# Attention scores on one core: PSUM buffers tied to engines, casts moved to GpSimd, whole memsets, transposes spread over five tiles

## The chip, the cores and the metric

One core of a Trainium2 chip. The metric is device time in microseconds (us) for one execution, median of several. Before: 204.12 us (204.04 to 204.3, 3 runs). "Faster" or "slower" needs 2%, about 4.1 us.

## The reference

```python
# q, k: (8, 8, 512, 64) float32
def reference(q, k):
    scale = 1.0 / np.sqrt(q.shape[-1])
    return (np.einsum('bhqd,bhkd->bhqk', q, k) * scale).astype(np.float32)
```

The inputs have 16.8 MB, the output 67.1 MB. All arithmetic on q and k is in bf16, sums and output are fp32.

## The kernel before

Four units (v) of two batches each; a unit has eight output tiles (n) of 128 x 8 x 512 fp32, 2 MB each. Each unit's k and q are loaded as one 2 MB tile apiece, cast to bf16, transposed on TensorE (PE) through PSUM, the buffer that TensorE writes to, copied to SBUF, the on-chip memory (kT, and qz with zeros in the half that the other head uses), and multiplied. The scores leave PSUM with the scale applied (an evacuation), by ScalarE (ACT) or VectorE (DVE) in turn, and are stored by one queue on SyncE (SP).

```python
    raw_pool = ctx.enter_context(tc.tile_pool(name="raw", bufs=3))
    ...
    out_pool = ctx.enter_context(tc.tile_pool(name="out", bufs=4))
    tpsum_pool = ctx.enter_context(tc.tile_pool(name="tpsum", bufs=2, space=bass.MemoryType.PSUM))
    psum_pool = ctx.enter_context(tc.tile_pool(name="psum", bufs=3, space=bass.MemoryType.PSUM))
    ...
    def evacuate(dst, src):
        nonlocal n_evac
        if n_evac % 2 == 0:
            pinned(nc.scalar.mul(out=dst, in_=src, mul=scale))
        else:
            pinned(nc.vector.tensor_scalar(out=dst, in0=src, scalar1=scale, ...))
        n_evac += 1

    def load_and_cast(v):
        both = []
        for src in (k_r, q_r):
            xf = raw_pool.tile([P, 2, J * D], f32, name="xf")
            nc.sync.dma_start(out=xf, in_=src[v])
            xb = bf_pool.tile([P, J, 2, D], bf16, name="xb")
            for s in range(2):
                if v == 0 and src is k_r:
                    copy = (nc.vector.tensor_copy, nc.scalar.copy)[s]
                else:
                    copy = nc.gpsimd.tensor_copy
                pinned(copy(out=xb[:, :, s, :], in_=xf[:, s].rearrange(...)))
            both.append(xb)
        return both
    ...
    for v in range(UNITS):
        ahead = transpose(v + 1, *cast[v + 1]) if v + 1 < UNITS else iter(())
        per_step = 3 if v == 0 else 1      # steps of the next unit's transposes per evacuation
        for n in range(N):
            take(ahead, 1)
            for _ in scores(v, n):         # two matmuls, one evacuation; the store after the fourth
                take(ahead, per_step)
```

`pinned` keeps an engine's instructions in this order. All loads are issued before all stores, on one queue. The fourth load waits until the first raw buffer has been cast.

Of the kernel before, what the change touches and what calls it, by code (L numbers as in the profile page):

```python
# [1 line left out]

# [5 lines left out]


@with_exitstack  # L10
def kernel(
    ctx: ExitStack,
    tc: tile.TileContext,
    q: bass.AP,
    k: bass.AP,
    out: bass.AP,
):






    nc = tc.nc
    B, H, S, D = q.shape
    scale = 1.0 / (D ** 0.5)
    P = 128
    UNITS = B // 2
    N = H
    M = P // (2 * H)  # L30
    R = S // M
    J = R // 2
    RO = 8
    U = S // RO
    JJ = J // RO
    IW = 8 // JJ

    f32 = mybir.dt.float32
    bf16 = mybir.dt.bfloat16

    q_r = q.rearrange("(v b) g (m j) d -> v (b g m) (j d)", b=2, j=R)
    k_r = k.rearrange("(v b) g (m j) d -> v (b g m) (j d)", b=2, j=R)
    out_r = out.rearrange("(v b) (n h) (u i) k -> v (b n) (h u) (i k)", b=2, h=2, i=RO)

    consts = ctx.enter_context(tc.tile_pool(name="consts", bufs=1))
    raw_pool = ctx.enter_context(tc.tile_pool(name="raw", bufs=3))
    bf_pool = ctx.enter_context(tc.tile_pool(name="bf", bufs=5))
    t_pool = ctx.enter_context(tc.tile_pool(name="t", bufs=2))
# [5 lines that stand above are left out]
    pinned = tc.keep_in_program_order  # L54

    n_evac = 0
    n_tp = 0

    def evacuate(dst, src):
        nonlocal n_evac  # L60
        if n_evac % 2 == 0:
            pinned(nc.scalar.mul(out=dst, in_=src, mul=scale))  # L62
        else:
            pinned(nc.vector.tensor_scalar(out=dst, in0=src, scalar1=scale, scalar2=None,  # L64
                                           op0=mybir.AluOpType.mult))
        n_evac += 1

    def half(h):
        return slice(h * D, (h + 1) * D)
# [6 lines that stand above are left out]
            nc.sync.dma_start(out=xf, in_=src[v])  # L76
            xb = bf_pool.tile([P, J, 2, D], bf16, name="xb")
            for s in range(2):
                if v == 0 and src is k_r:
                    copy = (nc.vector.tensor_copy, nc.scalar.copy)[s]  # L80
                else:
                    copy = nc.gpsimd.tensor_copy
                pinned(copy(out=xb[:, :, s, :], in_=xf[:, s].rearrange("p (j d) -> p j d", j=J)))  # L83
            both.append(xb)
        return both

    def clear(qz, h):

        nc.vector.memset(qz[half(h), :, :, (1 - h) * U:(2 - h) * U], 0.0)  # L89

    def rearrange(tp, pattern, dst):

        nonlocal n_tp
        copy = (nc.vector.tensor_copy, nc.scalar.copy)[n_tp % 2]
        n_tp += 1
        for s in range(2):
            src = tp[half(s)].rearrange(pattern, n=N, h=2)
            for h in range(2):
                pinned(copy(out=dst(s, h), in_=src[:, h]))  # L99
                yield  # L100

    def transpose(v, kb, qb):


        kT = t_pool.tile([P, N, M, 2, J], bf16, name="kT")
        qz = qzs[v % 2]
        ts[v] = (kT, qz)
        for j0 in range(0, J, 8):
            tp = tpsum_pool.tile([P, 8, P], bf16, name="tp")
            for j in range(8):  # L110
                pinned(nc.tensor.transpose(out=tp[:, j, :], identity=identity,  # L111
                                           in_=kb[:, j0 + j].rearrange("p s d -> p (s d)")))
            yield
            yield from rearrange(tp, "d j (n h m) -> d h n m j",
                                 lambda s, h: kT[half(h), :, :, s, j0:j0 + 8])
        for i0 in range(0, RO, IW):
            tp = tpsum_pool.tile([P, IW, JJ, P], bf16, name="tp")
            for i in range(IW):
                for jj in range(JJ):
                    pinned(nc.tensor.transpose(out=tp[:, i, jj, :], identity=identity,  # L120
                                               in_=qb[:, RO * jj + i0 + i].rearrange("p s d -> p (s d)")))
            yield
            yield from rearrange(tp, "d i jj (n h m) -> d h i n m jj",
                                 lambda s, h: qz[half(h), i0:i0 + IW, :, h * U:(h + 1) * U]
                                 .rearrange("d i n (m s jj) -> d s i n m jj", s=2, jj=JJ)[:, s])

    def scores(v, n):

        kT, qz = ts[v]
        o = out_pool.tile([P, RO, S], f32, name="o")  # L130
        for i in range(0, RO, 2):
            ps = psum_pool.tile([P, 2, S], f32, name="ps")
            for w in range(2):
                pinned(nc.tensor.matmul(out=ps[:, w, :], lhsT=qz[:, i + w, n, :],  # L134
                                        rhs=kT[:, n].rearrange("d m s j -> d (m s j)"),
                                        start=True, stop=True))
            evacuate(o[:, i:i + 2, :], ps)
            yield
        src = o.rearrange("p i k -> p (i k)")
        nc.sync.dma_start(out=out_r[v, n], in_=src)  # L140

    def take(steps, count):
        for _ in range(count):
            next(steps, None)

    identity = consts.tile([P, P], dtype=bf16)
    make_identity(nc, identity)
    qzs = [consts.tile([P, RO, N, P], bf16, name=f"qz{n}") for n in range(2)]
    for qz in qzs:
        for h in range(2):  # L150
            clear(qz, h)
    cast = [load_and_cast(v) for v in range(UNITS)]

    ts = {}
    for _ in transpose(0, *cast[0]):
        pass
    for v in range(UNITS):
        ahead = transpose(v + 1, *cast[v + 1]) if v + 1 < UNITS else iter(())

        per_step = 3 if v == 0 else 1  # L160
        for n in range(N):
            take(ahead, 1)
            for _ in scores(v, n):
                take(ahead, per_step)
        for _ in ahead:
            pass


# [1 line left out]
_INS = ['q', 'k']  # L170
_OUTS = [((8, 8, 512, 512), 'float32')]


# [23 lines left out]
```

## Time and profile before

| | before |
|---|---|
| time, median | 204.12 us |
| span in the profile | 202.3 us |
| DVE / PE / ACT / POOL busy | 64% / 52% / 51% / 13% |
| DMA queue, share of 16 engines | 97.7% |
| moved | 83.89 MB in 40 transfers of 2 MB |
| evacuations waiting for a store to free a tile | 79.4 us (ACT 50.9, DVE 28.5) |

A busy share is an average over the span. The row of 40 slices: the digit is the busy share in tenths, and 9 stands for 90% or more.

### The profile page before, as it was taken

The numbers are of one execution on the slowest core, as the hardware profiler recorded it, in microseconds if no ns is written. First come the engines' busy times: TensorE is split into PE (matmuls) and PEld (weight loads), VectorE is DVE, ScalarE is ACT, GpSimd is POOL, SyncE is SP. The second block draws the span as 40 slices with busy tenths as digits, with TensorE's granted clock in tenths as the row PEclk, the third lists the DMA queues.
The fourth block names the chain that finished last, engine by engine and source line by source line (L and its number), as shares of the span: only waits on it lengthen the run. The fifth ranks groups of instructions, "written<-read, shape, count | busy, mean of one in ns | idle before, by whom it ended". The sixth has DMA issues, their size and how long they took to land.

```text
span 202.3 us, 1549 instructions
## 1 busy us (share of the span) xinstructions
PE 106.1 (52%) x512; PEld 50.2 (25%) x512; DVE 129.6 (64%) x133; ACT 102.5 (51%) x130; POOL 26.8 (13%) x20
## 2 busy tenths in 40 slices
PE   0045557755854755858575575656564677642000
PEld 0034424432211322423222233223121222210000
DVE  6875669987765686878787788777544455553000
ACT  2254457967654448484756666574833344442000
POOL 1037775756000000000000000000000000000000
PEclk9999999978799699797979787896969655695555
DMA  6999999999999999999999999999999999999991
GB/s 214 428 441 428 424 441 421 424 395 434 437 421 434 432 423 431 434 428 428 437 424 431 431 424 434 434 428 431 434 428 428 431 434 428 428 437 429 416 447 75
DMA packets 5768, 83.99 MB, mean 415 GB/s; under 512 B 640, under 2 KB 640, under 8 KB 640
## 3 DMA queue, kind: packets, MB, share of 16 engines
q1 hardware_dynamic: 5760, 83.89, 97.7%
q8 instruction: 4, 0.07, 0.1%
q14 instruction: 4, 0.03, 0.0%
HBM read 16.78 MB, written 67.11 MB: 415 GB/s over the span
## 4 chain that ended last, share of the span: by engine, by line
DMA 52%; ACT 13%; DVE 13%; PE 10%; issue 2%; ACTq 0%; DVEq 0%; SPq 0%
DMA out_dram<-o 52%; ACT o L62 6%; DVE o L64 5%; PE ps L134 5%; ACT qz L99 4%; DVE qz L89 3%; ACT kT L99 3%; PE tp L120 3%; DVE kT L99 3%; PE tp L111 2%; DVE xb L83 1%; DVE qz L99 1%; ACTq L62 0%; DVEq L64 0%; SPq L140 0%
## 5 line engine op out<-in xcount | busy, mean ns | idle before, releaser
L134 PE MATMUL ps<-kT,qz 128*128 128x512 bf16 x256 | 87.3, 470 | 52.4 <-ACT o L62 43.3
L64 DVE TENSOR_SCALAR o<-ps 128x1024 f32<-128x1024 f32 x64 | 78.2, 1225 | 44.1 <-DMA out_dram<-o 28.5
L62 ACT ACTIVATE o<-ps 128x1024 f32<-128x1024 f32 x64 | 63.5, 1022 | 64.3 <-DMA out_dram<-o 50.9
L134 PEld LDWEIGHTS <-qz 128*128 128x128 bf16 x256 | 28.6, 115 | 98.6 <-issue 87.2
L83 POOL CAST xb<-xf 128x2048 bf16<-128x2048 f32 x14 | 26.1, 1893 | 21.5 <-DMA xf<-in_q_dram 18.1
L99 DVE COPY kT<-tp 64x512 bf16<-64x512 bf16 x32 | 22.0, 687 | 4.3 <-PE tp L111 3.8
L99 DVE COPY qz<-tp 64x512 bf16<-64x512 bf16 x32 | 22.0, 687 | 4.2 <-PE tp L120 3.7
L111 PE MATMUL tp<-identity,xb 128*128 128x128 bf16 x128 | 13.0, 267 | 17.0 <-DVE xb L83 11.1
L99 ACT COPY kT<-tp 64x512 bf16<-64x512 bf16 x32 | 18.5, 578 | 5.0 <-PE tp L111 4.7
L99 ACT COPY qz<-tp 64x512 bf16<-64x512 bf16 x32 | 18.5, 577 | 4.2 <-PE tp L120 3.9
L120 PE MATMUL tp<-identity,xb 128*128 128x128 bf16 x128 | 13.3, 271 | 8.1 <-ACT qz L99 4.9
L111 PEld LDWEIGHTS <-xb 128*128 128x128 bf16 x128 | 11.2, 122 | 21.3 <-ACT xb L83 11.1
L120 PEld LDWEIGHTS <-xb 128*128 128x128 bf16 x128 | 11.5, 123 | 12.6 <-issue 9.7
L89 DVE MEMSET qz<- 64x2048 uint32 x4 | 7.1, 1765 | 2.6 <-issue 1.4
L83 ACT CAST xb<-xf 128x2048 bf16<-128x2048 f32 x1 | 1.9, 1898 | 6.7 <-DMA xf<-in_k_dram 6.7
L83 ACT ACT_TABLE_LOAD x1 | 1.3, 1283 | 0.7 <-PEq L181 0.7
L83 DVE CAST xb<-xf 128x2048 bf16<-128x2048 f32 x1 | 1.2, 1227 | 0.0
masks.py:199 POOL TENSOR_SCALAR_AFFINE_SELECT identity<-identity 128x128 bf16<-128x128 bf16 x1 | 0.3, 292 | 0.1
masks.py:197 POOL MEMSET identity<- 128x128 bf16 x1 | 0.2, 205 | 0.3 <-POOLq L181 0.3
L181 POOL MEMSET const-float32-0.0<- 128x1 f32 x1 | 0.1, 98 | 0.2 <-issue 0.2
L181 POOL MEMSET const-bfloat16-1.0<- 128x1 bf16 x1 | 0.1, 101 | 0.0
L181 POOL MEMSET const-uint8-127<- 128x1 uint8 x1 | 0.1, 101 | 0.0
(1 smaller groups left out, 0.1 us busy)
## 6 DMA issues: line engine op xcount, KB each, us to landing
out_dram<-o SPq DMA_DIRECT2D x32, 2048.0 KB, 16.1
xf<-in_k_dram SPq DMA_DIRECT2D x4, 2048.0 KB, 11.3
xf<-in_q_dram SPq DMA_DIRECT2D x4, 2048.0 KB, 12.3
```

The lines of the kernel that those rows point to most:

```text
L62: pinned(nc.scalar.mul(out=dst, in_=src, mul=scale))
L64: pinned(nc.vector.tensor_scalar(out=dst, in0=src, scalar1=scale, scalar2=None, op0=mybir.AluOpType.mult))
L83: pinned(copy(out=xb[:, :, s, :], in_=xf[:, s].rearrange("p (j d) -> p j d", j=J)))
L89: nc.vector.memset(qz[half(h), :, :, (1 - h) * U:(2 - h) * U], 0.0)
L99: pinned(copy(out=dst(s, h), in_=src[:, h]))
L111: pinned(nc.tensor.transpose(out=tp[:, j, :], identity=identity, in_=kb[:, j0 + j].rearrange("p s d -> p (s d)")))
L120: pinned(nc.tensor.transpose(out=tp[:, i, jj, :], identity=identity, in_=qb[:, RO * jj + i0 + i].rearrange("p s d -> p (s d)")))
L134: pinned(nc.tensor.matmul(out=ps[:, w, :], lhsT=qz[:, i + w, n, :], rhs=kT[:, n].rearrange("d m s j -> d (m s j)"), start=True, stop=True))
L181: nc = _bacc.Bacc("TRN2", target_bir_lowering=False, num_devices=1)
```

## The change

Its intent, as it reads: with three PSUM buffers and two engines in strict turn, each buffer is freed by ACT one time and by DVE the next. In the pattern 0, 2, 3 of six, buffer 0 is always freed by ACT, buffer 1 always by DVE, and only buffer 2 changes. GpSimd (POOL) takes over the two casts of the first k, the only ones that ACT and DVE still had. The zeros are written by two large memsets in place of four half ones. The second unit's transposes are spread over five output tiles in place of four.

```diff
-        if n_evac % 2 == 0:
+        if n_evac % 6 in (0, 2, 3):
...
-                if v == 0 and src is k_r:
-                    copy = (nc.vector.tensor_copy, nc.scalar.copy)[s]
-                else:
-                    copy = nc.gpsimd.tensor_copy
-                pinned(copy(out=xb[:, :, s, :], ...))
+                pinned(nc.gpsimd.tensor_copy(out=xb[:, :, s, :], ...))
...
-        for h in range(2):
-            clear(qz, h)                 # memset of 64 partitions, half of the columns
+        nc.vector.memset(qz, 0.0)
...
-        per_step = 3 if v == 0 else 1
+        per_step = 2 if v == 0 else 1
```

More of the change, by code (lines that the diff above doesn't have):

```diff
@@ L78, in load_and_cast @@
             for s in range(2):
-                if v == 0 and src is k_r:
-                    copy = (nc.vector.tensor_copy, nc.scalar.copy)[s]
-                else:
-                    copy = nc.gpsimd.tensor_copy
-                pinned(copy(out=xb[:, :, s, :], in_=xf[:, s].rearrange("p (j d) -> p j d", j=J)))
+                pinned(nc.gpsimd.tensor_copy(out=xb[:, :, s, :],
+                                             in_=xf[:, s].rearrange("p (j d) -> p j d", j=J)))
             both.append(xb)
         return both
-    def clear(qz, h):
-        nc.vector.memset(qz[half(h), :, :, (1 - h) * U:(2 - h) * U], 0.0)
     def rearrange(tp, pattern, dst):
```

## The prediction

> **What bounds the kernel now.** I read the page's shares first: DVE is the busiest engine at 64% of the span, ACT has 51%, PE 52%, POOL 13%. None is close to full, so I turned to the two lines of 40 slices that belong to the transfers, and to the queue:
>
> ```profile
> DMA  6999999999999999999999999999999999999991
> GB/s 214 428 441 428 424 441 421 424 395 434 437 421 434 432 423 431 434 428 428 437 424 431 431 424 434 434 428 431 434 428 428 431 434 428 428 437 429 416 447 75
> q1 hardware_dynamic: 5760, 83.89, 97.7%
> ```
>
> From the second slice to the last but one the 16 DMA engines are at 90% or more, at about 430 GB/s, through the loads, the change from loads to stores, and the stores. One queue holds 97.7% of the 16 engines' whole span. There is no stage in which the transfers wait for the compute engines. The time is therefore bytes over rate plus two edges. All 40 transfers (8 loads, 32 stores) have 2 MB. Four loads that land one after another start casts at 8.68, 13.58, 18.48 and 23.38 us, so one transfer takes 4.90 us. 40 x 4.90 = 196 us, or 195 us as 83.89 MB at 430 GB/s. In front lie some 1.7 us until the first byte moves (98 GB/s in the first 2 us), behind some 3 to 4 us in which the last of the 16 engines runs out (360 GB/s at 197 to 198 us, 115, 66, then 16 GB/s at 200 to 201 us). That makes 200 to 202, beside a span of 202.3 and a time of 204.12.
>
> Next, who waits for whom among the evacuations:
>
> ```profile
> L64 DVE TENSOR_SCALAR o<-ps 128x1024 f32<-128x1024 f32 x64 | 78.2, 1225 | 44.1 <-DMA out_dram<-o 28.5
> L62 ACT ACTIVATE o<-ps 128x1024 f32<-128x1024 f32 x64 | 63.5, 1022 | 64.3 <-DMA out_dram<-o 50.9
> ```
>
> Both evacuating engines stand idle mostly until a store has freed an output tile: compute waits for the queue, the right way round for a kernel bound by transfers. "PE ps <- ACT o 43.3 us" in the list of waits looks like the target of the change's PSUM pairing, but it lies behind those same stores.
>
> The only place where a change of compute could reach the time is the first 55 us. So I read the start, and when the queue is fed:
>
> ```profile
> 7.91 1.76 DVE L89 MEMSET qz<- 64x2048 uint32 x1 [0.47 <-issue]
> 8.68 1.90 ACT L83 CAST xb<-xf 128x2048 bf16<-128x2048 f32 x1 [6.66 <-DMA xf<-in_k_dram]
> 9.71 1.23 DVE L83 CAST xb<-xf 128x2048 bf16<-128x2048 f32 x1
> 11.02 0.33 SPq L76 DMA_DIRECT2D xf<-in_q_dram  x1
> ...
> 17.33 0.33 SPq L76 DMA_DIRECT2D xf<-in_k_dram  x1
> 22.23 0.33 SPq L76 DMA_DIRECT2D xf<-in_q_dram  x1
> 27.14 0.33 SPq L76 DMA_DIRECT2D xf<-in_k_dram  x1
> 32.04 0.33 SPq L76 DMA_DIRECT2D xf<-in_q_dram  x1
> 34.34 28.70 SPq L140 DMA_DIRECT2D out_dram<-o  x7
> ```
>
> The fourth load is issued at 11.02, when both halves of the first input are cast and its raw buffer is free. At that moment the second load has 2.5 us to go and the third another 4.9, so the engines have work until 18.4. The first store is issued at 34.34, while two loads are queued that only begin to be used at 39.05 and 45.17. Windows of the queue give stores at 34.34, 40.84, 48.24, 52.52, 55.62, 58.14, 62.70 us.
>
> **What the Trainium skill says.** "DMA: Bandwidth & Descriptors", Specifications, gives a fabric ceiling of 435 GB/s for the 16 engines. The trace agrees: 428 to 437 in most slices; nothing is left above it. "SBUF — State Buffer", Who interferes with whom, says that DMA never contends with a compute engine, and that GpSimd and VectorE can block one another only where VectorE runs a two-port mode or reads two SBUF inputs. The trace agrees as far as it goes: all 14 GpSimd casts take 1889 to 1894 ns, though VectorE works beside them. "VectorE: DVE Perf Modes", Zero memsets can be issued as uint32 (trn2), says a memset costs a cycle per element. The row here says 1765 ns for 2048 words, but the next begins 2.23 us later, which fits one 0.96 GHz cycle per word (2.13 us) and 0.1 us over; I work with 2.23.
>
> **The change, part by part.**
>
> (1) GpSimd casts the first k. Removed: one ACT cast (1.90 us) and one DVE cast (1.23). Added: two GpSimd casts in a row, 2 x 1.89, with the gap between as in the others 3.73 us. They start at 8.68, when k has landed, and end at 12.41, instead of 10.94. So the first transposes and the fourth load move from 11.05 to about 12.5: 1.45 us later. For the load that is no loss, since work is queued until 18.4. GpSimd is free again at 12.4, and the next input lands at 13.58, so its later casts don't move. It needs 3.73 us per load and loads come every 4.90.
>
> (2) The memsets. Four of 64x2048 words become two of 128x4096. By the cycle-per-word reading, two times 4.27 + 0.1 = 8.7 us in place of 4 x 2.23 = 8.9: done near 9.95 instead of 10.1 us (an estimate). VectorE no longer casts and is next needed for the first kT copy, about 13.5 us. Worth nothing.
>
> (3) The evacuations alternate by 0, 2, 3 of six on ACT: buffers 0, 2, 0 on ACT and 1, 1, 2 on DVE. Still 64 and 64, so engine time is unchanged. A tile's four evacuations become ADAA, DDAD, AADD. Worst is DDAD with three on DVE, 3 x 1.23 = 3.7 us, beside two at 2.45. From a freed tile to its store the kernel now needs 59.61 to 62.70, 3.1 us; I allow 4.3. At that time three more stores of 4.87 us are queued, 14.6 us, less some 3 us by which the slowest engine trails. Slack about 11 us at the release, about 7 at the issue.
>
> (4) Two steps per evacuation instead of three in the first unit. The second unit's transposes have 8 groups of 1 + 4 = 5 steps, 40 in all. A tile takes 1 + 4x3 = 13 steps now, so they end in the fourth tile; with 1 + 4x2 = 9 they end in the fifth. Nothing is added. By the third store's issue there are 18 + 7 = 25 steps done instead of 26 + 10 = 36: some nine copies of 0.6 us fewer on two engines, 2.7 us.
>
> Sum at the critical place: first store 34.3 + 1.45 - 1 (three to four copies fewer) = about 35; second about 40; third 48.2 + 1.45 - 2.7 = about 47. To keep every DMA engine fed, the first must be issued by about 41 (the earliest engines leave the loads near 42), the second by 46, the third by 51. The least slack goes from about 2.8 us (third store, before) to about 4. So all of it lies beside a full queue, and the change on the path is 0.
>
> **The rivals.** First, a hole in the loads: if GpSimd's first casts were blocked by the memsets, or the bigger memsets took twice my estimate, GpSimd would start near 15, free the first buffer near 19 and leave the queue dry for 2 to 3 us: 206 to 207. For it: GpSimd and DVE share ports, and the cast at 8.68 does overlap the last memset by about 1.3 us. Against it: the memset row has no sign of a two-port rate, and the slack of 6 us swallows a delay of 1.3. Second, a hole at the first stores: the pinned order puts three ACT evacuations and copies on one engine in the first tile; if that cost over 6 us, the time would rise by the excess. The copies and evacuations of a tile sum to 4 to 5 us on either engine, so I don't believe it. Third, a gain: less waiting of PE on ACT, a faster steady state. It would be real in a kernel bound by evacuation; here tiles come free every 4.87 us whatever the engines do, so it gives 0. Fourth, another layout of the tail or of instruction fetches in the same DMA engines (0.1 MB) may shift the last store by a few tenths either way.
>
> **Range and chances.** The path is unchanged, so I predict the time before, 204.1. The three runs before span 0.26 us; with the fourth rival a few tenths are likely, and the first would add some. 203.6 to 204.9. For faster by 2%, 4.1 us would have to come out of a queue that is full; I give 1%. For slower by 2%, a hole of over 4 us must open, more than the first rival makes; 1%. The rest is the same.
>
> **What would show it.** Right: the line of 40 DMA slices again without a digit under 9 in the middle; the fourth load at about 12.5 us and the fifth at 17.3; the first store near 35, the third before 48; evacuations still waiting for stores for tens of us; store releases every 4.87 us. Wrong: a DMA slice of 8 or less near 17 to 20 us or 42 to 52 us, GpSimd casts over 1.9 us, or evacuating engines that wait for PE and not for stores in the steady part.

## The result, and the profile after

204.5 us (204.33 to 204.62, 4 runs) beside 204.08 (204.0 to 204.3, 4 runs) of before in the same rounds: ratio 1.0018, 95% interval 1.0001 to 1.0036. Executions over 1.5% slower than the fastest of the same kernel are left out of the means. A ratio is the mean time of one kernel's fast runs over that of the other's of the same rounds, so it is not quite the ratio of the medians.

The page of the changed kernel, its rows for the transfers and the evacuations:

```profile
DMA  6999999999999999999999999999999999999991
GB/s 214 430 440 424 430 440 421 417 392 437 434 421 440 429 419 440 427 427 437 427 427 437 424 427 440 424 430 437 421 434 440 417 430 437 417 440 437 414 440 68
q1 hardware_dynamic: 5760, 83.89, 97.6%
...
L65 DVE TENSOR_SCALAR o<-ps 128x1024 f32<-128x1024 f32 x64 | 76.6, 1221 | 45.5 <-DMA out_dram<-o 29.5
L63 ACT ACTIVATE o<-ps 128x1024 f32<-128x1024 f32 x64 | 63.6, 1023 | 62.9 <-DMA out_dram<-o 51.3
```

The row of DMA shares is the same, digit by digit. The last two lines are read from the right: ACT still stood idle 51.3 us, and DVE 29.5, until a store had freed an output tile.

Its start, by time (start us, duration us, engine, line, operation):

```profile
1.66 3.47 DVE L144 MEMSET qz<- 128x4096 uint32 x1 [1.66 <-PEq L174]
5.93 3.47 DVE L144 MEMSET qz<- 128x4096 uint32 x1 [0.80 <-issue]
8.71 3.73 POOL L80 CAST xb<-xf 128x2048 bf16<-128x2048 f32 x2 [7.41 <-DMA xf<-in_k_dram]
12.46 0.33 SPq L77 DMA_DIRECT2D xf<-in_q_dram  x1
12.49 1.62 PEld L105 LDWEIGHTS <-xb 128*128 128x128 bf16 x16 [12.49 <-POOL xb L80]
```

GpSimd casts for 3.73 us, the fourth load goes out at 12.46 in place of 11.02, and the transposes begin at 12.49. And the first stores of the changed kernel:

```profile
35.79 0.35 SPq L134 DMA_DIRECT2D out_dram<-o  x1
41.75 0.34 SPq L134 DMA_DIRECT2D out_dram<-o  x1
46.98 2.09 SPq L134 DMA_DIRECT2D out_dram<-o  x2
```

Before, they stood at 34.34, 40.84, 48.24 and 52.52 us. So the first two are some 1 us later, the next two 1.3 and 3.8 us earlier. None of it changes by more than 0.1 us when bytes move: by the packets' records in the traces, 63.80 MB were still to be moved at 50 us before, and 63.83 MB after.

Where are the 0.4 us, if they are any? In the traces the spans differ by 0.2 us. At the end, the SP queue's own waits show this in the kernel before:

```profile
SPq L192 <- PEq L192: 0.6, 2, 0.4
```

and this in the changed one (total, times, longest):

```profile
SPq L185 <- PEq L185: 0.8, 2, 0.6
```

The last store lands at 201.48 us before and at 201.51 after, by the traces. So the 0.2 us of the span lie in the engines' meeting at the end of the program, after the last store. The experiments come back to it.

### The profile page after: what moved, and what is told of

It is laid out like the page before. It is cut to its first block, busy times and chain, and to the rows that moved or that the text cites. A ratio compares the mean times of both kernels' runs of the same rounds, so it can differ in the third digit from the quotient of the medians.

```text
span 202.5 us, 1539 instructions
## 1 busy us (share of the span) xinstructions
PE 105.7 (52%) x503; PEld 50.1 (25%) x512; DVE 126.3 (62%) x130; ACT 100.2 (49%) x129; POOL 30.5 (15%) x22
## 4 chain that ended last, share of the span: by engine, by line
DMA 50%; ACT 14%; DVE 11%; PE 10%; issue 3%; POOL 2%; DVEq 1%; ACTq 0%; SPq 0%
DMA out_dram<-o 46%; DVE o L65 7%; ACT o L63 7%; PE ps L128 5%; ACT qz L93 5%; DMA xf<-in_k_dram 4%; PE tp L105 3%; DVE kT L93 2%; PE tp L114 2%; ACT kT L93 2%; POOL xb L80 2%; DVE qz L93 1%; DVEq L185 1%; ACTq L63 0%; DVEq L65 0%
## 5 line engine op out<-in xcount | busy, mean ns | idle before, releaser
L65 DVE TENSOR_SCALAR o<-ps 128x1024 f32<-128x1024 f32 x64 | 76.6, 1221 | 45.5 <-DMA out_dram<-o 29.5
L63 ACT ACTIVATE o<-ps 128x1024 f32<-128x1024 f32 x64 | 63.6, 1023 | 62.9 <-DMA out_dram<-o 51.3
L80 POOL CAST xb<-xf 128x2048 bf16<-128x2048 f32 x16 | 29.8, 1893 | 17.6 <-DMA xf<-in_k_dram 11.8
L105 PE MATMUL tp<-identity,xb 128*128 128x128 bf16 x128 | 13.4, 273 | 18.4 <-POOL xb L80 12.5
L105 PEld LDWEIGHTS <-xb 128*128 128x128 bf16 x128 | 11.7, 126 | 22.6 <-POOL xb L80 12.5
L114 PE MATMUL tp<-identity,xb 128*128 128x128 bf16 x128 | 12.4, 259 | 6.7 <-DVE kT L93 3.4
L144 DVE MEMSET qz<- 128x4096 uint32 x2 | 6.9, 3472 | 2.5 <-PEq L174 1.7
```

Source lines behind the costliest of these rows:

```text
L80: pinned(nc.gpsimd.tensor_copy(out=xb[:, :, s, :], in_=xf[:, s].rearrange("p (j d) -> p j d", j=J)))
L105: pinned(nc.tensor.transpose(out=tp[:, j, :], identity=identity, in_=kb[:, j0 + j].rearrange("p s d -> p (s d)")))
L114: pinned(nc.tensor.transpose(out=tp[:, i, jj, :], identity=identity, in_=qb[:, RO * jj + i0 + i].rearrange("p s d -> p (s d)")))
L144: nc.vector.memset(qz, 0.0)
```

## The experiments

The chip's "before" varied between 203.93 and 204.5 us over these jobs, so a difference of 0.2% is near what can be seen. Every kernel below was correct unless it says otherwise.

### Each part alone (5 rounds each)

My theory: the queue is full, so every part is worth nothing. Rivals: the later first store costs time; the pairing or the earlier stores gain some. Each kernel is the one before with one hunk of the diff.

GpSimd casts the first k too:

```diff
-                if v == 0 and src is k_r:
+                if False:
```

> The kernel before with one part of the change: GpSimd casts the first k too. Theory (queue full, all delays covered): first store about 1.5 us later than 34.3, time within 0.2 us of before, 204.1. If the 0.4 us of the whole change come from ACT's end of program (its last drain came 0.3 us later in the trace after, while the last store landed at the same 201.5 us), then the part that takes one ACT instruction away may carry it: 204.3 to 204.5. Rival (a later first store costs time): 204.1 plus a part of 1.5 us, with a dip in the DMA row near 42 us.

Measured: 204.18 us (204.05 to 204.35), ratio 1.0002 (0.9989 to 1.0014). The first store went out at 35.81, 1.5 us later as expected, with no cost.

The pattern:

```diff
-        if n_evac % 2 == 0:
+        if n_evac % 6 in (0, 2, 3):
```

> The kernel before with the 0, 2, 3 of six pattern alone. Theory: 204.1 within 0.2, evacuations still wait for stores about 80 us in all. Rival (pairing of PSUM buffers with engines speeds the steady part): 202 or less.

Measured: 204.08 us (203.95 to 204.37), ratio 0.9997 (0.9984 to 1.0011). No gain in the steady part; evacuations waited 83.9 us for stores, where about 80 was expected. The first store moved to 35.90, 1.6 us later, which I had not expected: the first tile now has three of its four evacuations on ACT.

The memsets:

```diff
-        for h in range(2):
-            clear(qz, h)
+        nc.vector.memset(qz, 0.0)
```

> The kernel before with whole memsets alone. Theory: 204.1 within 0.2; DVE's cast of the first k starts at about the same time, 9.7 to 10.1 us.

Measured: 204.02 us (203.97 to 204.02), ratio 0.9992 (0.998 to 1.0005). DVE's cast of the first k began at 9.32 us, before the 9.7 to 10.1 that I expected (9.71 in the kernel before), and the first store went out at 33.88, 0.46 us earlier. That gained nothing either.

The steps:

```diff
-        per_step = 3 if v == 0 else 1
+        per_step = 2 if v == 0 else 1
```

> The kernel before with 2 steps in place of 3 alone. Theory: 204.1 within 0.2; first store about 33.3 us, third about 45.5 us, a longer queue and no gain. Rival (earlier stores gain time): 203 or less.

Measured: 204.02 us (203.92 to 204.22), ratio 0.9994 (0.9982 to 1.0007). The third store moved from 48.24 to 44.81 us and the fourth from 52.52 to 49.19, and not even that gained anything. The first moved to 34.64, 0.3 us later and not the 1 us earlier that I had put down.

So no part moves the time by more than 0.1% alone, and none shows the 0.4 us of the whole. The longer meeting at the end (0.8 in place of 0.6 us) isn't in any of the four either. It is in all four traces that have the whole change with ACT's number of instructions untouched (the changed kernel, and s_cast2, s_cast3 and h_after below), and in neither of the two that alter that number (s_copy2, a_all_dve). It thus appears to be a property of the combined program, 0.2 us long; what in the program makes it was not isolated, and the other 0.2 us are within what the kernel before varies.

### The transfers without the computation (3 rounds, wrong result)

The pool of output tiles also shrinks from four buffers to one for each of two names (not shown).

```diff
+    filled = [out_pool.tile([P, RO, S], f32, name=f"filled{n}") for n in range(2)]
+    for t in filled:
+        nc.vector.memset(t, 0.0)
     for v in range(UNITS):
         for n in range(N):
-            (transposes, matmuls, evacuations, and the store of the result)
+            nc.sync.dma_start(out=out_r[v, n], in_=filled[n % 2].rearrange("p i k -> p (i k)"))
```

> Wrong result on purpose: the same 8 loads with GpSimd's casts (the first k still on DVE and ACT) and the same 32 stores, of two tiles of zeros; no transposes, matmuls or evacuations. Theory (bytes over rate bound both kernels): 201 to 204.2, at most 2% under before, and that is all that any change of compute could gain. If the slowest of the 16 engines trails because of instruction fetches, the tail is shorter here and the time nearer 201.5. Rival (compute costs time somewhere): well under 200.

Measured: 201.44 us (201.33 to 201.6) beside 204.01, ratio 0.9874 (0.986 to 0.9889). Nearly all arithmetic is gone, and 1.3% with it. That is about the most that any change of the computation could have gained with these transfers in this order: the intended gain had no room. Windows of one us at its end (the last two columns are the share of the 16 DMA engines and GB/s; PE and its loads have no columns, as they do nothing; a packet, 16 KB here, is counted whole in the window in which it starts):

```profile
196.00:197.00 1.00, 0.00 (x0) 0.00 (x0) 0.00 (x0) 1.00 0.96 410
197.00:198.00 1.00, 0.00 (x0) 0.00 (x0) 0.00 (x0) 1.00 0.66 279
198.00:199.00 1.00, 0.00 (x0) 0.00 (x0) 0.00 (x0) 1.00 0.00 0
```

and the same of the kernel before:

```profile
197.00:198.00 1.00, 0.00 (x0) 0.00 (x0) 0.00 (x0) 0.00 (x0) 0.00 (x0) 0.50 0.84 360
198.00:199.00 1.00, 0.00 (x0) 0.00 (x0) 0.00 (x0) 0.00 (x0) 0.00 (x0) 0.50 0.27 115
199.00:200.00 1.00, 0.00 (x0) 0.00 (x0) 0.00 (x0) 0.00 (x0) 0.00 (x0) 0.50 0.15 66
200.00:201.00 1.00, 0.00 (x0) 0.00 (x0) 0.00 (x0) 0.00 (x0) 0.00 (x0) 0.50 0.04 16
```

Without the computation all DMA engines end within the same us; with it a few trail for 3 us. So the 2.6 us between the two kernels become visible in this ragged end, but part of them was lost earlier: at 196 us the kernel before still has 1.09 MB to move and this one 0.83 MB, which is 0.6 us at 430 GB/s. The traces' records of single packets say where. From 55 to 196 us the kernel before has seven instruction fetches in the same engines (0.31 us each for 8 KB, 0.88 to 0.95 for 16 KB), and just eight of its 3695 data packets took over 0.69 us in place of the usual 0.61, each of them next to a fetch; this kernel has no fetch and no such packet there. The fetches took 3.9 us of engine time, and the data packets 5.6 us beyond 0.61 each (0.7 here): together 9.5 us over 16 engines, about the 0.6 us. The changed kernel has seven fetches there too. That the other 2.0 us come from a few engines bearing most of this is likely but not shown, as the records do not say which engine moved a packet, and much else was taken away with the fetches.

### All evacuations on one engine (3 rounds)

Does the balance of the evacuating engines matter at all? The changed kernel with

```diff
-        if n_evac % 6 in (0, 2, 3):
+        if False:
```

> The changed kernel with all 128 evacuations on DVE. A tile then needs 4 x 1.22 = 4.9 us of DVE, as much as its store takes, plus the copies of the next unit: DVE is busy 6.9 + 44 + 128 x 1.22 = 207 us in all, and cannot start before 13.5 us. Theory (engines bind only beyond the queue's rate): 218 to 224, DVE above 90%, DMA row no longer full. Rival (engines never bind here): 204.5.

Measured: 226.84 us (226.7 to 227.01), ratio 1.112 (1.1101 to 1.1138), 3 us above the range, and DVE at 88%, a little under the 90% expected. Its rows:

```profile
PE 119.0 (53%) x512; PEld 52.2 (23%) x512; DVE 197.8 (88%) x194; ACT 38.4 (17%) x65; POOL 30.6 (14%) x22
...
DVE  6646759999999999999999999999999999999900
...
DMA  6999999995699998869686978879686999999994
```

Here the DVE row has the 9s and the DMA row has holes. This is what the page looks like when evacuation binds; neither kernel of the change looks so. (The durations of DVE's rows do add up to the 207 us that I had counted, but rows overlap: 128 evacuations of 1217 ns on average keep it busy for 148.6 us and not 155.8. What I left out is the stores still queued when DVE ends.)

### Delaying the loads (3 rounds each)

The prediction rests on slack: the fourth load may come 1.4 us later because the queue has work until 17 to 18 us. I delayed it further, by repeating the first k's casts in the changed kernel, twice in all:

```diff
-                pinned(nc.gpsimd.tensor_copy(out=xb[:, :, s, :], ...))
+                for _ in range(2 if v == 0 and src is k_r else 1):
+                    pinned(nc.gpsimd.tensor_copy(out=xb[:, :, s, :], ...))
```

> The changed kernel with the first k's two casts done twice over: first raw buffer free at 16.2 us, the queue has work until 17.6. Theory: no hole, 204.5 within 0.3. Rival (any delay of the first cast shows): 208.

Measured: 206.16 us (206.04 to 206.33), ratio to before 1.0098 (1.0081 to 1.0115): 1.7 us over the 204.5 of the changed kernel (which was timed in another job), where I had expected none. Three times in all (`range(3 ...)`):

> The changed kernel with the first k's two GpSimd casts done three times over: the first raw buffer is free at 8.7 + 3 x 3.73 = 19.9 us, when the queue ran dry at about 17.6. Theory: a hole of 20.0 + 1.0 - 17.6 = 3.4 us in the loads, time 207.4 to 208.4, the rest unchanged. Rival (lost load time is made up later): 204.5.

Measured: 209.37 us (209.12 to 209.55), ratio 1.0261 (1.0246 to 1.0277): 4.9 us more, where I had expected 3.4. Half-us windows of this kernel, in the same columns as before with PE, PEld, DVE, ACT and POOL ahead of clock, DMA share and GB/s:

```profile
16.50:17.00 0.50, 0.00 (x0) 0.00 (x0) 0.00 (x0) 0.00 (x0) 0.50 (x1) 1.00 1.15 492
17.00:17.50 0.50, 0.00 (x0) 0.00 (x0) 0.00 (x0) 0.00 (x0) 0.50 (x1) 1.00 0.16 66
...
20.50:21.00 0.50, 0.50 (x7) 0.50 (x6) 0.00 (x0) 0.00 (x0) 0.50 (x1) 1.00 0.00 0
21.00:21.50 0.50, 0.50 (x8) 0.50 (x6) 0.24 (x1) 0.00 (x0) 0.50 (x1) 1.00 2.53 492
21.50:22.00 0.50, 0.50 (x6) 0.30 (x3) 0.49 (x2) 0.00 (x0) 0.50 (x2) 1.00 0.32 66
22.00:22.50 0.50, 0.07 (x1) 0.00 (x0) 0.50 (x1) 0.39 (x1) 0.50 (x1) 1.00 0.56 164
22.50:23.00 0.50, 0.00 (x0) 0.00 (x0) 0.49 (x2) 0.49 (x2) 0.50 (x1) 1.00 0.70 295
23.00:23.50 0.50, 0.00 (x0) 0.00 (x0) 0.49 (x2) 0.49 (x2) 0.50 (x1) 1.00 1.07 459
```

Read these windows with care: as a packet counts where it starts, a share can be 2.53, and 492 followed by 66 GB/s is not a burst and a fall. The packets' records show fifteen packets that start between 21.1 and 21.5 us and take 0.78 to 1.96 us each, where a packet in the full queue takes 0.61; no new one starts until they end. The last packets before the hole start by 17.3 and end on average near 17.4, the last at 17.9; I had put 17.6. The load is issued at 20.16, and its first packet starts at 21.11, 0.95 us later. The slow first packets, twenty of them, lose 14 us over 16 engines, 0.9 us each. Counted over 17 to 23 us: 541 KB moved in place of 6 x 430 = 2580, which is 2039/430 = 4.7 us lost, the measured 4.9. So a load that meets an empty queue costs about a us beyond the gap itself.

The double cast is the milder case of the same: its fourth load is issued at 16.22, some 1.2 us before the queue is dry, and its first packets are slow all the same (up to 1.49 us each):

```profile
16.50:17.00 0.50, 0.50 (x8) 0.50 (x6) 0.00 (x0) 0.00 (x0) 0.50 (x1) 1.00 1.07 459
17.00:17.50 0.50, 0.50 (x7) 0.50 (x6) 0.18 (x1) 0.00 (x0) 0.50 (x1) 1.00 0.34 131
17.50:18.00 0.50, 0.50 (x6) 0.37 (x4) 0.50 (x1) 0.00 (x0) 0.50 (x2) 1.00 1.73 361
18.00:18.50 0.50, 0.14 (x2) 0.00 (x0) 0.49 (x2) 0.32 (x1) 0.50 (x2) 1.00 0.24 66
```

By the bytes moved, 1.2 to 1.4 us are lost here, the rest of the 1.7 in the change from loads to stores. So the slack of the fourth load ends before 16.2 and not near 17; the change's 12.46 is still well inside, as its window from 16 to 18 us shows: 434 GB/s, and no dip.

### Delaying the first store (3 rounds)

The changed kernel with the first unit's eight groups of PSUM copies done twice:

```diff
+        first = n_tp < 8
...
-                pinned(copy(out=dst(s, h), in_=src[:, h]))
+                for _ in range(2 if first else 1):
+                    pinned(copy(out=dst(s, h), in_=src[:, h]))
```

> The changed kernel with the first unit's PSUM copies of transposes done twice each: about 9 us later first store, 44 to 46 us, while the loads run out near 42.5. Theory (slack at the first store is about 5 us, the rest shows): hole of 3 to 4 us, time 207 to 209. Rival (large slack, the whole delay covered): 204.5. Rival (no slack): 213.

Measured: 209.72 us (209.56 to 210.15), ratio 1.0283 (1.0267 to 1.0298), 5.2 us over the changed kernel. The first store was issued at 45.76, inside the expected 44 to 46. Windows:

```profile
41.00:41.50 0.50, 0.50 (x3) 0.16 (x2) 0.49 (x2) 0.20 (x1) 0.50 (x1) 1.00 1.15 492
41.50:42.00 0.50, 0.50 (x3) 0.22 (x2) 0.32 (x1) 0.50 (x1) 0.24 (x1) 1.00 0.09 33
...
46.00:46.50 0.50, 0.46 (x3) 0.10 (x1) 0.50 (x2) 0.49 (x2) 0.00 (x0) 1.00 0.00 0
46.50:47.00 0.50, 0.00 (x0) 0.00 (x0) 0.50 (x2) 0.49 (x2) 0.00 (x0) 1.00 1.23 524
```

By the packets' records the loads' last packets end on average near 41.8 us (the last at 42.3), and the store's first start at 46.6 and take the usual 0.61 us from the first on: a hole of 4.8 us, which comes through to the end whole. Nothing is made up later. This store's bytes moved 0.85 us after its issue, so the changed kernel's first one could have gone out at 41.8 - 0.85 = 41.0 us, and its 35.79 has 5.2 us to spare. Counted the other way, 10.0 us of delay cost 5.2, so 4.8 were covered. The prediction had "by about 41". Its limits for the second and third store were not tested.

### Half of the bytes stored (3 rounds each, wrong result)

Is the pairing worth something where compute binds? Every second row of an output tile stored, 50.3 MB in place of 83.9:

```diff
-        src = o.rearrange("p i k -> p (i k)")
-        nc.sync.dma_start(out=out_r[v, n], in_=src)
+        odd = out_r[v, n].rearrange("p (i k) -> p i k", i=RO)[:, 1::2, :]
+        nc.sync.dma_start(out=odd, in_=o[:, 1::2, :])
```

The kernel before with this edit:

> Wrong result on purpose: the kernel before with every second of the eight rows of an output tile stored, 50.3 MB in all in place of 83.9. Theory: the queue needs only 50.3/430 = 117 us, so compute binds: DVE is busy 130 us, the start takes about 30 us: 155 to 170 us, evacuating engines wait for PE and one another and not for stores. Rival (not bound by bytes): over 195.

Measured: 155.78 us over four runs, one of them slow (157.97; the three fast ones took 154.68 to 156.09, and the ratio uses these), ratio to the kernel before 0.7614 (0.7583 to 0.7645). As expected, the evacuating engines wait for PE (ACT 21.2 us) and no longer for stores. The changed kernel with this edit:

> The same for the changed kernel. If pairing PSUM buffers with engines has a worth where compute binds: 2 to 8% faster than h_before. If it has none even there: within 1% of h_before.

Measured: 154.39 us (154.31 to 155.08), ratio to before 0.7571 (0.7554 to 0.7587). And the kernel before with this edit and the pattern alone:

> h_before with the 0, 2, 3 of six pattern alone: shows whether a difference between h_after and h_before comes from the pairing (as h_after within 1%) or from casts, memsets and steps (as h_before within 1%).

Measured: 156.72 us (155.83 to 158.02), ratio to before 0.7683 (0.7639 to 0.7727). By the ratios the changed kernel is at 0.7571/0.7614 = 0.994 of h_before, and the pattern alone at 1.009: neither is a gain of 2%, with intervals of 0.2 to 0.6% either side of each ratio, and the pairing alone gains nothing. The waits of one profiled run each fit that (h_pattern's was the slowest of its four, 158.02 us). In h_before PE waits for a PSUM buffer:

```profile
PE ps L134 <- ACT o L62: 22.4, 31, 2.7
...
PE ps L134 <- DVE o L64: 4.3, 10, 1.7
```

and in h_pattern:

```profile
PE ps L134 <- ACT o L62: 18.6, 29, 1.8
...
PE ps L134 <- DVE o L64: 10.9, 21, 1.0
```

The pairing takes 3.8 us of waiting for ACT away and adds 6.6 us of waiting for DVE. And here DVE is at the bound: 19.65 of the 20 us from 60 to 80 are busy in h_before, and 19.59 in h_after. How buffers are dealt out does not make that engine's work less.

## Why the prediction was right

**The bound.** "There is no stage in which the transfers wait for the compute engines" held: the row of DMA shares is unchanged, and without the computation the time falls by only 1.3%. Two readings need care. The row hides what is shorter than its slices of 5 us: at the change from loads to stores, 40 to 42 us, the rate was 360 GB/s before and 328 after, but 344 and then 295 without the computation too, so this dip isn't made by the computation. And slices of 441 to 447 GB/s, above the 435 beyond which "nothing is left", can come from counting a packet where it starts. The sum of bytes over rate plus edges (200 to 202 us) was a little loose: it counts the bytes of the last 3 to 4 us (0.56 MB, 1.3 us) twice and leaves out the 1.3 us between the last bytes at 201.0 and the end of the span. Without the computation the span is 199.6, just under it, as most of that tail is gone. The other signs came as well: the fifth load at 17.35 us, and ACT's evacuations that wait for a store start at 88.71, 93.58, 98.44 and 103.31, 4.86 to 4.87 us apart.

**The casts.** The first transposes and the fourth load at "about 12.5 us": 12.49 and 12.46. Alone, no cost. GpSimd's casts took 1893 ns each and 3.73 us a pair, as predicted.

**The memsets.** The cycle-per-word reading gave 4.37 us per memset; the second starts 4.27 us after the first (4096 words, 0.96 per ns), though its row says 3472 ns. But it does not fit throughout: with the memsets alone, DVE's cast starts 3.39 us after the start of the second memset, and where the estimate has the memsets done "near 9.95 instead of 10.1 us", that cast starts at 9.32 instead of 9.71. How long a memset holds VectorE is thus open. Worth nothing, as predicted.

**The pattern and the steps.** Worth nothing, as predicted, and for the reason given: evacuations wait for stores. But the times of the first stores were partly right by luck. The prediction had first 35, second 40, third 47 and they were 35.79, 41.75 and 46.98. Its term "- 1 (three to four copies fewer)" was wrong: alone the steps make the first store 0.3 us later, and the pattern, whose three ACT evacuations in the first tile the second rival names but to which the sum gives no cost, 1.6 us later. The parts do not add: 34.34 + 1.47 (cast) + 1.56 (pattern) + 0.30 (steps) - 0.46 (memset) would be 37.2, and the whole gives 35.79.

**The slack.** At the first store it held (41.0 beside "about 41"). At the loads its size was wrong: "the engines have work until 18.4" took the landing for the end of the bytes, which is near 17.4 on average, and left out that a load's first packet starts some 0.95 us after its issue and that its first packets are slow. So "the slack of 6 us" was under 3.8 us, as issuing at 16.22 in place of 12.46 cost 1.7 us. A load issued at 20.16 cost 4.9 us; the first rival has a hole of "2 to 3 us" for a buffer freed near 19, so 3 to 4 there. The change stays clear of both, so the predicted time was not touched.

**A few tenths.** The fourth rival allowed for them. Half of the 0.4 us is a longer meeting of the engines at the end, in all four traces of the whole program in which ACT's instructions are untouched; its cause in the program is open.

## What to carry to other kernels

Before you value a change of the computation, look whether the row of transfers has a digit under 9: if it has none, the change has little to gain (here at most 1.3%), and the question is how far it moves the first load and the first store towards the moment when the queue is dry. Count that moment from the last bytes moved and not from the landing, and give a load ample lead: here 1.2 us was too little and 4.9 us enough, and nothing between was tried. None of the three delays beyond the slack was made up later; and a pattern that deals out buffers more neatly gained nothing even where one engine's own work was the bound. When you read short windows of transfers, remember that a packet counts whole where it starts.

## What the Trainium skill lacked or had wrong

- "DMA: Bandwidth & Descriptors", Where 436 GB/s comes from, says that for transfers between HBM and SBUF the HBM side, about 358 GB/s, binds. Read alone, that sentence is wrong for this program on one core: it moved 414 to 447 GB/s, loads and stores alike, in every slice of both kernels but the first, the last and the one at the change from loads to stores (395 and 392). The page's own note just before that section, which ties the 358 to both cores of a pair streaming, and the fabric figure of 435 fit.
- The same page gives a first-byte latency of about 0.6 us for queues such as SP's. A store to an idle queue had its first packet 0.85 us after the start of its issue (45.76 to 46.61), a load 0.95 us (20.16 to 21.11), which is near. What the page does not have: the first packets of a load into an idle queue took 0.78 to 1.96 us in place of 0.61 and cost about 0.9 us per engine, while a store's took 0.61 from the first on.
- "VectorE: DVE Perf Modes", Zero memsets can be issued as uint32 (trn2), has a cycle per element, which fits one number here and not another: for 4096 words the profile's row says 3472 ns, the next memset starts 4.27 us after the first, but with the memsets alone a cast starts 3.39 us after the start of the second. That section doesn't say that the row is not the cost; the skill elsewhere times a memset from the rows around it, without a figure for the gap.
- "GPSIMD Engine Reference", Key points, puts VectorE at about twice GpSimd's speed for elementwise work. For the cast of 2048 fp32 to bf16 it was 1227 against 1893 ns, a ratio of 1.54.
- No page has the 0.2 us by which the engines' meeting at the end of a program can differ between two builds of nearly the same work.
